# Half and transpose buffers of the latent heads in freed V memory, and the chunked outputs loaded once, in a hybrid encoder layer

## Chip, cores and metric

The kernel runs on one core of one Trainium2 chip. The metric is the device time of one execution in microseconds (us); lower is better.

## What is computed

One layer of a streaming encoder on a sequence of 1024 tokens with 1024 channels, in float32. Two groups of attention heads work on the same normalized input, their outputs are concatenated and projected, and a gated MLP follows:

```python
h = modulate(rmsnorm(x, g_attn_norm), sh_a, sc_a)
q_lat, kv_lat, k_rope, ca_qkv = split(h @ w_in)
# A: 8 latent heads, 96 wide keys, chunk-causal over all earlier keys
q = rmsnorm(q_lat) @ w_q_up;  k_nope, v = split(rmsnorm(kv_lat) @ w_kv_up)
o_mla = mla_attention(rope(rmsnorm(q)), rope(rmsnorm([k_nope, k_rope])), v)
# B: 8 chunked heads, 64 wide, a band of 9 chunks of 64 keys, relative bias
o_ca = chunk_attention(rmsnorm(cq), rmsnorm(ck), cv, rel_bias)
x = x + g_a * (concat([o_mla, o_ca]) @ w_out)
h = modulate(rmsnorm(x, g_mlp_norm), sh_m, sc_m)
gate, val = split(causal_dwconv(h @ w_up, conv_w, conv_b))
x = x + g_m * ((silu(gate) * val) @ w_down)
```

## The kernel before

The work is tiled by 128 tokens (8 tiles). Products that need float32 accuracy run as three matmuls on a high and a low part of each operand (`gemm3`): ACT makes the high part (`hi_of`, L75), POOL or DVE subtracts it for the low part (`lo_of`, L82).

A scheduler orders the instructions of each engine when the program is built, by the order in which they are issued in the source and by priorities (`tc.high_priority`); each engine then runs its own list in order and waits on semaphores. All DMAs are issued by SP's queue, transposes too, in one list. Buffers come from pools: tiles with one `tag` share `bufs` places, and a new tile waits until the last reader of the place is done.

The main loop goes over 32 units of four query tiles each: first the chunked heads (`ca_unit`, tile names ending in `c`), then the latent heads (`mla_unit`, names in `m`; `m13` is group 1, head 3). For each query tile `Unit.scores` computes q k^T into PSUM (tag S, two places), takes the row extreme on DVE (L674) and the exponential on ACT (L680) into a tile `P` (three places up to 640 keys, else a page tile with six). The probabilities are then scaled and split into two float16 halves side by side in a tile `hl`: the high half on POOL (L71), the low half on DVE (L700). One DMA transpose (L702) writes both halves, turned, into a tile `PT`. A tile of up to 640 keys is one piece, a longer one is cut in two (512 and the rest). `hl` has the tag HL with three places, `PT` the tag PT with three places. Three tiles later (`DEPTH`) `Unit.values` multiplies V with the turned halves (L713), and after four tiles ACT and DVE evict the sum and SP stores it to `oT_d` in DRAM (L720 to L722).

V of the chunked heads lies in tiles with the tag `v16` (six places of 1024 float16 for each partition), which `f_v` fills.

Between these steps the loop draws pieces of other work from a list of fillers, so that PE has matmuls while a unit waits: `pace` takes as many as a cost account asks for. The last filler is `f_oca`. It multiplies the outputs of the chunked heads (blocks 4 to 7 of `oT_d`) with their rows of `w_out` and stores the partial result to `part_d`. `load_wo` stages each weight tile through `qtile` (tag sq, two places), as the result tiles `co` are too. The input tiles come from `rtile` (tag R, four places).

After the loop, `load_wo` loads the other half of `w_out` through the same staging places, and a loop over the eight token tiles adds the latent heads' outputs (L870 to L897). The MLP stage follows.

Of the kernel before, what the change touches and what calls it, by code (L numbers as in the profile page):

```python
# [13 lines left out]
F32R = mybir.dt.float32r  # L14
F16 = mybir.dt.float16
# [8 lines left out]
P = 128  # L24
D = 1024
S = 1024
NT = S // P
# [13 lines left out]
P_BUFS, HL_BUFS, PT_BUFS, TB = 3, 3, 3, 1  # L41
# [21 lines left out]
def layer_kernel(ctx, tc, I, out):  # L63
    nc = tc.nc
    pe, act, dve, pool, sp = nc.tensor, nc.scalar, nc.vector, nc.gpsimd, nc.sync

    def f32(ap):
        return ap.bitcast(F32)
# [4 lines left out]
    def hi_of(eng, o, i):  # L73
        if eng == "a":
            act.activation(o, i, AF.Copy)  # L75
        elif eng == "p":
            pool.tensor_scalar(o, i, 1.0, 0.0, op0=MUL, op1=ADD)
        else:
            dve.tensor_copy(o, i)

    def lo_of(eng, o, i, hi):
        (pool if eng == "p" else dve).tensor_tensor(o, i, f32(hi), op=SUB)  # L82
# [3 lines left out]
    oT_d = dram.tile([ND, P, S], F32, name="oT_d")  # L86
# [37 lines left out]
    apg = att_pg.__enter__()  # L124
# [9 lines left out]
    def rtile(name, shape=(P, 512), dt=F32):  # L134
        return apg.tile(list(shape), dt, name=name, tag="R", bufs=4)

    def qtile(name):
        return apg.tile([P, 512], F32, name=name, tag="sq", bufs=2)
# [4 lines left out]
    def pgtile(shape, dt, name):  # L143
        return apg.tile(shape, dt, name=name, tag="pg", bufs=6)
# [13 lines left out]
    def gemm3_f(pt, pairs, step=GSTEP):  # L158
        n, w = len(pairs), pt.shape[-1]
        for i0 in range(0, n, step):  # L160
            part = pairs[i0:i0 + step]
            if len(trail) > LAG:
                with tc.issue_after(trail[-1 - LAG]):
                    gemm3(pt, part, i0 == 0, i0 + step >= n)
            else:
                gemm3(pt, part, i0 == 0, i0 + step >= n)
            yield 3 * len(part) * max(107, w / 2.4 + 2.5)
# [68 lines left out]
    for d in range(ND):  # L236
# [7 lines left out]
        pt = ps.tile([P, 512], F32, name=f"p_ada{d}", tag="mm", bufs=2)  # L244
# [86 lines left out]
    at = att.__enter__()  # L331
# [177 lines left out]
    def g4(shape, dt, name):  # L509
        return G["4"].tile(shape, dt, name=name, tag="G4", bufs=8)  # L510
# [72 lines left out]
    def load_wo(k0, n, he, le):  # L583
        ws = []
        for k in range(k0, k0 + 4):
            raw = qtile(f"wor{k}_{n}")
            sl = slice(n * 512, (n + 1) * 512)
            sp.dma_start(raw[:], I["w_out"][k * P:(k + 1) * P, sl])
            w = g4([P, 2, 512], F32R, f"wo{k}_{n}")
            hi_of(he, w[:, 0], raw[:])  # L590
            lo_of(le, w[:, 1], raw[:], w[:, 0])
            ws.append(w)
        return ws

    def f_oca():
        for n in range(2):
            ws = load_wo(4, n, "a", "p")
            for t in range(NT):
                lo = rtile(f"cl{t}_{n}", (P, 4, P), F32R)
                hi = rtile(f"ch{t}_{n}", (P, 4, P), F32R)  # L600
                sp.dma_start(f32(lo[:]), oT_d[4:8, :, t * P:(t + 1) * P].rearrange("k p t -> p k t"))
                hi_of("a", hi[:], f32(lo[:]))
                lo_of("p", lo[:], f32(lo[:]), hi[:])
                pt = ps.tile([P, 512], F32, name=f"oc{t}_{n}", tag="mm", bufs=2)
                yield from gemm3_f(pt[:], [(hi[:, k], lo[:, k], ws[k][:, 0], ws[k][:, 1]) for k in range(4)])
                o = qtile(f"co{t}_{n}")
                act.activation(o[:], pt[:], AF.Copy)
                sp.dma_start(part_d[t][:, n * 512:(n + 1) * 512], o[:])
# [16 lines left out]
    class Unit:  # L625
# [7 lines left out]
        def scores(u, i):  # L633

            qpg, kpgs = u.pages()
            bias = u.bias() if u.band else None
            lo = max(0, i - 4) if u.band else 0
            n = (i - lo + 1) * P
            nm = f"{u.nm}_{i}"
            rsum = cst.tile([P, 1], F32, name=f"rs{nm}", tag="rsum", bufs=4)  # L640
            ri = cst.tile([P, 1], F32, name=f"ri{nm}", tag="ri", bufs=4)
            with tc.high_priority(offset=OFF_S):
                s = ps.tile([P, 1024], F32, name=f"s{nm}", tag="S", bufs=2)
                n0 = max(0, min(4, i + 1) - lo) * P
                n1 = n - n0
                c0 = 512 - n0 if n1 else 0
                segs = [(c0, lo * P, n0, 0)] if n0 else []
                if n1:
                    segs.append((512, max(lo, 4) * P - 512, n1, 1))
                q = slice((i % 4) * P, (i % 4 + 1) * P)  # L650
                rs_ = slice(u.base, u.base + u.rows)
                for a in range(2):
                    for c, ko, w, kh in segs:
                        for b in range(2 - a):
                            last = pe.matmul(s[:, c:c + w], qpg[rs_, a, q], kpgs[kh][rs_, b, ko:ko + w],  # L655
                                             start=(a == 0 and b == 0), stop=(a == 1))
                trail.append(last.ins)
                sv = s[:, c0:c0 + n]
                m = cst.tile([P, 1], F32, name=f"m{nm}", tag="m", bufs=4)
                if u.band:  # L660
                    if i >= 4:
                        dve.memset(sv[64:128, 0:64], BIG)
                    w = min(n, 256)
                    if n > 256:
                        m0 = cst.tile([P, 1], F32, name=f"m0{nm}", tag="m0", bufs=4)
                        dve.tensor_reduce(m0[:], sv[:, :n - 256], axis=AX.X, op=MIN)
                        init = m0[:]
                    else:
                        init = 3e38
                    dve.tensor_tensor_reduce(sv[:, n - w:n], sv[:, n - w:n], bias[:, 256 - w:256], 1.0, init,  # L670
                                             ADD, MIN, accum_out=m[:])
                else:
                    dve.memset(sv[0:64, n - 64:n], BIG)
                    dve.tensor_reduce(m[:], sv, axis=AX.X, op=MIN)  # L674
                pieces = [(0, n)] if n <= 640 else [(0, 512), (512, n)]
                if n <= 640:
                    pr = at.tile([P, 640], F32, name=f"P{nm}", tag="P", bufs=P_BUFS)
                else:
                    pr = pgtile([P, 1024], F32, f"P{nm}")
                act.activation(pr[:, :n], sv, AF.Exp, bias=m[:], scale=-1.0, accum_out=rsum[:, 0:1])  # L680
            with tc.high_priority(offset=OFF_P):
                dve.reciprocal(ri[:], rsum[:, 0:1])
                dve.tensor_scalar(ri[:], ri[:], PSCALE, None, op0=MUL)  # L683
                u.pt[i] = []
                for x, (p0, p1) in enumerate(pieces):
                    w = p1 - p0
                    hl = at.tile([P, 1280], F16, name=f"hl{nm}_{x}", tag="HL", bufs=HL_BUFS)
                    pp = pr[:, p0:p1]
                    cnt[0] += 1
                    mode = (MODE_C if u.band else MODE_M)[cnt[0] % 4]  # L690
                    if mode == "2":
                        scale_pool(pp, pp, ri[:])
                        act.activation(hl[:, :w], pp, AF.Copy)
                        pool.tensor_tensor(hl[:, w:2 * w], pp, hl[:, :w], op=SUB)
                    else:
                        if mode == "1":
                            scale_pool(hl[:, :w], pp, ri[:])
                        else:
                            act.activation(hl[:, :w], pp, AF.Copy, scale=ri[:])
                        dve.scalar_tensor_tensor(hl[:, w:2 * w], pp, ri[:], hl[:, :w], op0=MUL, op1=SUB)  # L700
                    tt = at.tile([P, 10, P], F16, name=f"PT{nm}_{x}", tag="PT", bufs=PT_BUFS)
                    sp.dma_start_transpose(tt[:, :2 * w // P, :], hl[:, :2 * w])  # L702
                    u.pt[i].append((tt, lo + p0 // P, w // P))
            return sum(3 * max(107, w / 2.4) for _, _, w, _ in segs)
# [20 lines left out]
    cnt = [0]  # L725
# [88 lines left out]
    for n in range(len(tiles) + DEPTH):  # L814
        if n < len(tiles):
            u, i = tiles[n]
# [4 lines left out]
        if n >= DEPTH:  # L821
            u, i = tiles[n - DEPTH]
# [47 lines left out]
    for t in range(NT):  # L870
        lo = gb.tile([P, 4, P], F32R, name=f"ol{t}", tag="ol", bufs=3)
        hi = gb.tile([P, 4, P], F32R, name=f"oh{t}", tag="oh", bufs=3)
# [7 lines left out]
        pt = ps2.tile([P, 1024], F32, name=f"op{t}", tag="op", bufs=3)  # L880
# [268 lines left out]
```

## Time and profile before

| | us |
|---|---|
| median of three runs | 1467.54 |
| the three runs | 1464.54 to 1467.68 |
| span of the profiled execution, first to last instruction | 1461.0 |

The page gives no other time of the profiled execution than its span; the median lies 6.5 us above it. In the page PE is busy for 87% of the span, DVE 70%, POOL 53%, ACT 42%. The scores of the latent heads run from 426 to 655 us and their last products end at 676 us.

In the profile's rows, "A <- B: total, times, longest" means that A waited for B. In a group row the columns are line, engine, operation, tiles written and read, shapes and count, then busy time in us and mean ns of one, then the idle time of the engine just before and what ended it. SPq is SP's queue of DMA issues. PEclk is the granted TensorE clock as a share of full speed, and the DMA share is the mean busy share of the 16 DMA engines.

### The profile page before, as it was taken

How to read it: one execution, taken by the hardware profiler on the slowest of the kernel's cores; microseconds unless marked ns; L12 is line 12 of the kernel's file. 1: busy time of each engine (PE TensorE's matmuls, PEld its weight loads, DVE VectorE, ACT ScalarE, POOL GpSimd, SP SyncE). 2: the span in 40 equal slices, each digit the busy share in tenths (PEclk: the TensorE clock that was granted, in tenths of full speed). 3: DMA queues.
4: the chain of work that ended last, by engine and by line, in shares of the span. 5: the costliest groups of instructions: out<-in, count | busy, mean ns of one | idle time of the engine just before them, and what ended most of it. 6: DMA issues, size and time to landing. Idle time of an engine off the chain costs nothing.

```text
span 1461.0 us, 20153 instructions
## 1 busy us (share of the span) xinstructions
PE 1273.7 (87%) x6836; PEld 1053.1 (72%) x6836; DVE 1028.2 (70%) x1830; ACT 611.7 (42%) x1190; POOL 780.0 (53%) x717
## 2 busy tenths in 40 slices
PE   3859989998867788885776999999999998999997
PEld 2749878886746666764555888788888887887885
DVE  6874776476798968772487887777777777566653
ACT  4544354343455545443273434334444433332331
POOL 5263554274555745444545555566555555665662
PEclk9979987999788899996887999999999999999998
DMA  7323547455522577869611323322222234446442
GB/s 282 134 71 75 131 113 150 126 122 116 115 64 45 127 153 161 175 139 270 223 72 63 111 100 108 109 87 87 87 87 87 77 137 162 151 144 237 148 142 101
DMA packets 218595, 185.94 MB, mean 127 GB/s; under 512 B 148086, under 2 KB 183034, under 8 KB 217468
## 3 DMA queue, kind: packets, MB, share of 16 engines
q1 hardware_dynamic: 218492, 184.66, 44.0%
q8 instruction: 54, 0.88, 0.2%
q14 instruction: 49, 0.40, 0.1%
HBM read 121.17 MB, written 28.84 MB: 103 GB/s over the span
## 4 chain that ended last, share of the span: by engine, by line
PE 39%; DMA 18%; DVE 16%; POOL 12%; issue 11%; ACT 3%; SPq 1%; DVEq 0%; POOLq 0%; ACTq 0%
POOL wds L82 5%; PE p L921 4%; PE p L923 4%; PE p L922 4%; DMA aw<-w_ada 4%; DMA PTm<-hlm 3%; DMA wu<-w_up 3%; PE sc L655 3%; PE dnp L1064 2%; PE dnp L1066 2%; PE dnp L1065 2%; PE sm L655 2%; DMA PTc<-hlc 2%; DVE adacc L243 2%; DMA cl<-oT_d 1%
## 5 line engine op out<-in xcount | busy, mean ns | idle before, releaser
L82 POOL TENSOR_TENSOR wds<-wd,wds 128x512 fp32r<-128x512 f32 x88 | 153.6, 1766 | 100.7 <-ACT wds L75 100.7
L82 POOL TENSOR_TENSOR wc<-ws,wc 128x512 fp32r<-128x512 f32 x22 | 65.4, 2975 | 134.7 <-ACT wc L75 134.7
L1054 DVE TENSOR_TENSOR wd<-wd,gmbc 128x1024 f32<-128x1024 f32 x44 | 69.4, 1577 | 80.7 <-DMA wd<-w_down 78.1
L1064 PE MATMUL dnp<-wds,g 128*128 128x512 f32 x308 | 119.9, 391 | 2.8 <-DVE xo L1072 2.3
L1066 PE MATMUL dnp<-wds,g 128*128 128x512 f32 x308 | 118.5, 390 | 3.8 <-DVE g L82 3.8
L75 ACT ACTIVATE wds<-wd 128x512 fp32r<-128x512 f32 x88 | 54.8, 624 | 157.8 <-PE dnp L1066 152.7
L1065 PE MATMUL dnp<-wds,g 128*128 128x512 f32 x308 | 119.6, 389 | 0.0
L71 POOL TENSOR_SCALAR hlm<-Pm,rim 128x512 f16<-128x512 f32 (+4 forms) x88 | 66.5, 760 | 58.1 <-DMA PTm<-hlm 37.0
L71 POOL TENSOR_SCALAR hlc<-Pc,ric 128x640 f16<-128x640 f32 (+2 forms) x64 | 45.6, 715 | 79.2 <-DVE ric L683 40.1
L700 DVE SCALAR_TENSOR_TENSOR hlm<-Pm,rim,hlm 128x512 f16<-128x512 f32 (+4 forms) x88 | 66.1, 758 | 23.3 <-POOL hlm L71 23.0
L1012 DVE TENSOR_TENSOR ws<-wu,wu 128x512 f32<-128x512 f32 x22 | 28.1, 1279 | 75.6 <-DMA wu<-w_up 75.6
L655 PE MATMUL sm<-mk,mq 96*128 96x512 f32 (+3 forms) x288 | 71.1, 378 | 10.3 <-ACT Pm L680 9.3
L82 DVE TENSOR_TENSOR g<-gr,g 128x512 fp32r<-128x512 f32 x44 | 71.0, 1616 | 11.4 <-ACT g L75 11.4
L998 DVE SCALAR_TENSOR_TENSOR u<-c,pk,u 128x1023 f32<-128x1023 f32 x44 | 77.4, 1765 | 1.8 <-ACT u L997 1.8
L1033 ACT ACTIVATE u<-u 128x1024 f32<-128x1024 f32 x22 | 23.4, 1063 | 132.0 <-DVE u L999 132.0
L713 PE MATMUL pvm<-PTm,vt 128*128 128x128 f16 x576 | 49.4, 239 | 33.5 <-DMA PTm<-hlm 28.6
L680 ACT ACTIVATE Pc<-sc,mc 128x640 f32<-128x640 f32 (+2 forms) x64 | 42.2, 659 | 86.2 <-DVE mc L670 61.7
L997 ACT ACTIVATE u<-c,pk 128x1024 f32<-128x1024 f32 x44 | 52.3, 1236 | 55.2 <-DVE c L1029 55.2
L430 DVE SCALAR_TENSOR_TENSOR aacc<-aw,cs,aacc 128x256 f32<-128x256 f32 x84 | 44.7, 532 | 43.5 <-DMA aw<-w_ada 42.9
L655 PE MATMUL sc<-k,q 64*128 64x512 f32 (+3 forms) x288 | 70.1, 372 | 5.3 <-ACT Pc L680 3.0
L713 PEld LDWEIGHTS <-vt 128*128 128x128 f16 x576 | 40.6, 108 | 46.3 <-issue 41.2
L1066 PEld LDWEIGHTS dnp<-wds,g 128*128 128x128 f32 x308 | 57.8, 188 | 17.1 <-DVE g L82 5.0
(366 smaller groups left out, 4308.0 us busy)
## 6 DMA issues: line engine op xcount, KB each, us to landing
wu<-w_up SPq DMA_DIRECT2D x44, 512.0 KB, 3.9
wd<-w_down SPq DMA_DIRECT2D x44, 512.0 KB, 4.4
aw<-w_ada SPq DMA_DIRECT2D x96, 128.0 KB, 2.3
g_d<-u SPq DMA_DIRECT2D x22, 512.0 KB, 2.6
gr<-g_d SPq DMA_DIRECT2D x44, 256.0 KB, 3.6
x<-x SPq DMA_DIRECT2D x16, 512.0 KB, 8.0
adaw<-w_ada_a SPq DMA_DIRECT2D x8, 1024.0 KB, 5.6
wq_r<-w_qk SPq DMA_DIRECT2D x32, 128.0 KB, 2.5
```

What stands on the lines that cost most here:

```text
L71: pool.tensor_scalar(o, i, s, 1.0, op0=MUL, op1=MUL)
L82: (pool if eng == "p" else dve).tensor_tensor(o, i, f32(hi), op=SUB)
L655: last = pe.matmul(s[:, c:c + w], qpg[rs_, a, q], kpgs[kh][rs_, b, ko:ko + w], start=(a == 0 and b == 0), stop=(a == 1))
L700: dve.scalar_tensor_tensor(hl[:, w:2 * w], pp, ri[:], hl[:, :w], op0=MUL, op1=SUB)
L713: last = pe.matmul(u.pv[:, c], u.vst(j), mov, start=(x == 0), stop=(x == len(todo) - 1))
L921: pe.matmul(pt, sh, pg[:, 0], start=(k == 0), stop=False)
L922: pe.matmul(pt, sh, pg[:, 1], start=False, stop=False)
L998: dve.scalar_tensor_tensor(u[:, 1:], c[:, :S - 1], pk[:, cv + 1:cv + 2], u[:, 1:], op0=MUL, op1=ADD)
L1054: dve.tensor_tensor(raw[:], raw[:], gmbc[:], op=MUL)
L1064: pe.matmul(pts[t][n], sh, w[n][:, 0], start=(j == 0), stop=False)
L1065: pe.matmul(pts[t][n], sh, w[n][:, 1], start=False, stop=False)
L1066: pe.matmul(pts[t][n], sl, w[n][:, 0], start=False, stop=(j == NF - 1))
```

## The change

`f_oca` loads and splits the weights of both column halves first, and its loop over token tiles stands outside: each tile is loaded and split once and used for both halves. In `Unit.scores`, tiles of 640 keys of a latent head are cut into 512 and 128 too, and every second piece of a latent head takes its `hl` and its `PT` from the tag `v16`, six places, instead of HL and PT. There are 96 pieces of latent heads then, not 88.

```diff
     def f_oca():
-        for n in range(2):
-            ws = load_wo(4, n, "a", "p")
-            for t in range(NT):
-                lo = rtile(f"cl{t}_{n}", (P, 4, P), F32R)
-                hi = rtile(f"ch{t}_{n}", (P, 4, P), F32R)
-                sp.dma_start(f32(lo[:]), oT_d[4:8, :, t * P:(t + 1) * P].rearrange("k p t -> p k t"))
-                hi_of("a", hi[:], f32(lo[:]))
-                lo_of("p", lo[:], f32(lo[:]), hi[:])
+        ws = [load_wo(4, n, "a", "p") for n in range(2)]
+        for t in range(NT):
+            lo = rtile(f"cl{t}", (P, 4, P), F32R)
+            hi = rtile(f"ch{t}", (P, 4, P), F32R)
+            sp.dma_start(f32(lo[:]), oT_d[4:8, :, t * P:(t + 1) * P].rearrange("k p t -> p k t"))
+            hi_of("a", hi[:], f32(lo[:]))
+            lo_of("p", lo[:], f32(lo[:]), hi[:])
+            for n in range(2):
                 pt = ps.tile([P, 512], F32, name=f"oc{t}_{n}", tag="mm", bufs=2)
-                yield from gemm3_f(pt[:], [(hi[:, k], lo[:, k], ws[k][:, 0], ws[k][:, 1]) for k in range(4)])
+                yield from gemm3_f(pt[:], [(hi[:, k], lo[:, k], ws[n][k][:, 0], ws[n][k][:, 1]) for k in range(4)])
...
-                pieces = [(0, n)] if n <= 640 else [(0, 512), (512, n)]
+                short = n <= (640 if u.band else 512)
+                pieces = [(0, n)] if short else [(0, 512), (512, n)]
...
-                    hl = at.tile([P, 1280], F16, name=f"hl{nm}_{x}", tag="HL", bufs=HL_BUFS)
+                    cnt[0] += 1
+                    spare = not u.band and cnt[0] % 2
+                    if spare:
+                        hl = apg.tile([P, 1024], F16, name=f"hl{nm}_{x}", tag="v16", bufs=6)
+                    else:
+                        hl = at.tile([P, 1280], F16, name=f"hl{nm}_{x}", tag="HL", bufs=HL_BUFS)
                     pp = pr[:, p0:p1]
-                    cnt[0] += 1
...
-                    tt = at.tile([P, 10, P], F16, name=f"PT{nm}_{x}", tag="PT", bufs=PT_BUFS)
+                    if spare:
+                        tt = apg.tile([P, 8, P], F16, name=f"PT{nm}_{x}", tag="v16", bufs=6)
+                    else:
+                        tt = at.tile([P, 10, P], F16, name=f"PT{nm}_{x}", tag="PT", bufs=PT_BUFS)
                     sp.dma_start_transpose(tt[:, :2 * w // P, :], hl[:, :2 * w])
```

## The prediction

> **What bounds the kernel now.** I read the page first (span, chain), then the stretches by time, then who waited for whom in the stretch that the change touches, then the shapes of its instructions, and last the timeline of its end. The page gives the span; the three runs have their median at 1467.54 us. The page has no other time for the profiled execution, so I count the 6.5 us between as lying around the span, and apply every change in us to the median.
>
> ```profile
> span 1461.0 us, 20153 instructions
> ```
>
> The stretches (columns: us, busy PE, PEld, DVE, ACT, POOL, granted clock, DMA share, GB/s):
>
> ```profile
> 100.00:200.00 100.00, 98.90 (x784) 89.63 (x783) 61.37 (x179) 40.80 (x96) 43.48 (x57) 1.00 0.44 101
> 200.00:300.00 100.00, 94.37 (x658) 82.59 (x657) 65.06 (x195) 41.09 (x106) 43.39 (x54) 0.85 0.55 130
> 470.00:655.00 185.00, 152.94 (x1026) 122.29 (x1024) 145.63 (x374) 92.74 (x199) 97.64 (x104) 0.92 0.70 149
> 655.00:682.00 27.00, 10.67 (x88) 9.01 (x87) 10.18 (x19) 7.88 (x14) 9.51 (x11) 0.62 0.91 212
> ```
>
> The diff touches only the latent heads and the partial output product beside them. Their body is 470 to 655 us, their drain 655 to 682. In the body PE is busy 152.9 of 185 us, so 32.1 us is the most that any rearrangement can win there; DVE at 145.6 is the next limit, only 7 us better. What PE waits for, and what stands behind it (us, times, longest), in the body:
>
> ```profile
> POOL hlm L71 <- DMA PTm<-hlm: 32.3, 24, 4.1
> DVE hlm L700 <- POOL hlm L71: 19.2, 21, 3.6
> ACT Pm L680 <- DVE hlm L700: 8.1, 5, 2.5
> PE sm L655 <- ACT Pm L680: 4.8, 6, 2.2
> PE pvm L713 <- DMA PTm<-hlm: 13.6, 17, 2.0
> PE oc L150 <- ACT ch L75: 3.6, 5, 1.1
> PE oc L150 <- ACT wo L75: 1.5, 1, 1.5
> SPq L702 <- PE pvm L713: 19.8, 20, 1.4
> ```
>
> The first four rows are one chain: POOL can't write the high half of the next probabilities until a transpose has emptied one of the three HL buffers; DVE waits for POOL's half, ACT for the P buffer that DVE frees, PE's scores for ACT. The last row is the second limit of three: SP can't start a transpose until PE's value products have read a PT buffer. Together they allow three pieces between POOL and PE, and a tile of over 640 keys has two. PE pays 13.6 us (value products waiting for a transpose) and 4.8 us (scores waiting for ACT), 18.4 of its 32.1 idle us.
>
> **The change part by part.** (1) Every second piece of a latent head takes its halves and its transpose from the six V buffers, so six pieces may be under way, not three. In the built order of the changed kernel the transpose of piece 13_6_0 waits for the products of 13_2_0, six pieces back; before, it waits for 13_4_0, three back. Both limits go. What is late next is not free: the probability buffers stay at three for up to 640 keys, PE's order is fixed, and DVE is at 79%. Bounds: 0 if the next limit binds at once, -18.4 us if all waits of both rows go. Going through PE's waits in time, most come shortly behind a POOL wait of the first row, as the last of these rows does behind the one before it; the first does not, POOL was late with other work there.
>
> ```profile
> 491.83 0.61 PE L713 MATMUL pvm<-PTm,vt 128*128 128x128 f16 x8 [1.75 <-DMA PTm<-hlm]
> 646.13 0.69 POOL L71 TENSOR_SCALAR hlm<-Pm,rim 128x512 f16<-128x512 f32 x1 [3.55 <-DMA PTm<-hlm]
> 648.65 0.61 PE L713 MATMUL pvm<-PTm,vt 128*128 128x128 f16 x8 [1.25 <-DMA PTm<-hlm]
> ```
>
> I take half of 18.4: **-9.2 us**.
>
> (2) Tiles of 640 keys become pieces of 512 and 128. One form of each operation becomes two:
>
> ```profile
> L71 POOL TENSOR_SCALAR hlm<-Pm,rim 128x640 f16<-128x640 f32 x8 | 7.6, 950 | 6.0 <-ACT kraw L564 2.5 <-DVE rim L683 2.2 <-DMA PTm<-hlm 1.2
> L71 POOL TENSOR_SCALAR hlm<-Pm,rim 128x512 f16<-128x512 f32 x40 | 34.6, 866 | 25.0 <-DMA PTm<-hlm 14.9 <-DVE rim L683 4.6 <-DVE sm L673 2.2
> L71 POOL TENSOR_SCALAR hlm<-Pm,rim 128x128 f16<-128x128 f32 x8 | 3.5, 437 | 2.0 <-DVE sm L673 1.7 <-DMA PTm<-hlm 0.2
> L700 DVE SCALAR_TENSOR_TENSOR hlm<-Pm,rim,hlm 128x640 f16<-128x640 f32 x8 | 7.0, 880 | 0.2 <-POOL hlm L71 0.2
> L700 DVE SCALAR_TENSOR_TENSOR hlm<-Pm,rim,hlm 128x512 f16<-128x512 f32 x40 | 34.1, 853 | 9.9 <-POOL hlm L71 9.8
> L700 DVE SCALAR_TENSOR_TENSOR hlm<-Pm,rim,hlm 128x128 f16<-128x128 f32 x8 | 3.2, 404 | 0.8 <-POOL hlm L71 0.8
> L702 SPq DMA_TRANSPOSE PTm<-hlm x88: 1167/1238/2220, 434.1 to 671.2; - x88
> DMA to landing us min/median/max: 2.3/3.3/4.7
> ```
>
> Eight times: POOL 866+437-950 = 0.35 us, DVE 853+404-880 = 0.38 us, SP one issue of 1.24 us. That is 2.8, 3.0 and 9.9 us of engine time, between 0 (all in idle time) and 3.0 (DVE's share on the path in full; SP's 9.9 is offset below). DVE idles 39 of the 185 us; I take a third: **+1.0**. PE's products stay ten for these tiles. [...]
>
> (3) The partial product loads and splits each chunked output once:
>
> ```profile
> L601 SPq DMA_DIRECT2D cl<-oT_d x16: 372/434/653, 493.9 to 636.7; - x16
> L75 ACT ACTIVATE ch<-cl 128x512 fp32r<-128x512 f32 x16 | 10.1, 628 | 23.7 <-DMA cl<-oT_d 20.9 <-DVE qn L470 2.8
> L82 POOL TENSOR_TENSOR cl<-cl,ch 128x512 fp32r<-128x512 f32 x16 | 21.9, 1368 | 28.6 <-ACT ch L75 26.3 <-PE mq_ps L615 2.2
> ```
>
> Eight of sixteen go: ACT 5.0 us, POOL 10.9 us, SP 8 x 0.43 = 3.5 us and 2 MB of reads. All of it is beside PE's work; what PE feels is its 3.6 us wait for ch. Bounds 0 and -3.6, half: **-1.8**. In return all eight weight tiles of w_out are loaded and split ahead of the first output tile, where the second four stood in the middle. PE's wait for them is 1.5 us now; twice the row, so **+1.5** more, from 0 to the price in the slower rival.
>
> (4) The drain. SP's order there (start, us):
>
> ```profile
> 654.62 0.59 SPq L588 DMA_DIRECT2D wor<-w_out  x1
> 657.52 4.25 SPq L702 DMA_TRANSPOSE PTm<-hlm  x3
> 662.49 0.39 SPq L588 DMA_DIRECT2D wor<-w_out  x1
> 670.36 0.57 SPq L588 DMA_DIRECT2D wor<-w_out  x1
> 671.19 1.25 SPq L702 DMA_TRANSPOSE PTm<-hlm  x1
> 684.64 0.33 SPq L588 DMA_DIRECT2D wor<-w_out  x1
> 681.65 0.80 PE L150 MATMUL op<-wo,oh 128*128 128x512 f32 x1 [5.69 <-ACT oh L75]
> 692.09 1.20 DVE L82 TENSOR_TENSOR wo<-wor,wo 128x512 fp32r<-128x512 f32 x1 [2.52 <-ACT wo L75]
> ```
>
> Now the transposes at 657.52 stand for a PT buffer. Without that wait they start at 655.2 and nine of them (one is the new piece) at 1.24 us end near 666.4, not at 672.4: the last value product comes some 6 us sooner. But the output projection that follows ends on the last weight tile, split at 692 to 693. The loads for it take turns in two staging buffers: from 670.36 to 684.64 five steps, 2.86 us each. In the changed order the second load no longer stands among the transposes (662.49) but behind all of them and two stores: about 668. Six steps of 2.86 put the last at 685, where it was. So the 6 us are won and lost again: between -6 and +2, I take **-0.5**.
>
> Sum: -9.2 + 1.0 - 1.8 + 1.5 - 0.5 = -9.0. Span 1452, median 1467.5 - 9.0 = **1458.5 us**. Everything after 705 us keeps its order.
>
> **The rivals.**
>
> [...] Chance 0.13.
>
> *The transfers are the bound*: six pieces under way only queue in the DMA engines.
>
> ```profile
> DMA packets 5154, 1.80 MB, mean 180 GB/s; under 512 B 4865, under 2 KB 4865, under 8 KB 5153
> q1 hardware_dynamic: 5153, 1.78, 96.6%
> ```
>
> These are 660 to 670 us: six transposes and three small transfers fill the 16 engines at only 180 GB/s. The body's mean share of 0.70 leaves room between bursts, and part 3 takes 2 MB away; inside bursts it may not. Then the gain is 0 to -3: about 1466. [...] Chance 0.15.
>
> *Slower: weights at the head of SP's queue.* The loads of the second four weight tiles now stand among the transposes of the second and third latent head (about 500 to 525 us), each waiting for POOL to free a staging buffer, with the transposes behind it.
>
> ```profile
> SPq L588 <- POOL wo L82: 4.9, 2, 2.9
> L82 POOL TENSOR_TENSOR wo<-wor,wo 128x512 fp32r<-128x512 f32 x12 | 17.7, 1480 | 12.3 <-ACT wo L75 12.3
> wor<-w_out SPq DMA_DIRECT2D x9, 256.0 KB, 3.3
> ```
>
> Four such waits at the longest seen, 2.9 us, are 11.6 us in which no transpose starts; PE meets its first product with them soon after and stands too. It decides if a load, its two halves (ACT's as for ch above) and POOL's queue take more than a turn of (3.3 + 0.6 + 1.5) / 2 = 2.7 us. With half of part 1 won: +11.6 - 4.6 = +7, 1474.5. For it: SP is held at such loads already. Against: the built order spreads those products over six tiles. Chance 0.21.
>
> *It does not do what it says*: the next limit (three P buffers, DVE) binds at once: 1467. Chance 0.06. The forecast keeps 0.45, with 1452 to 1464 as its own range.
>
> **How the numbers follow.** A measurement here tells 0.2%, 3 us, from no change. Faster: 0.45 + 0.13 and a part of the DMA case, 0.60. Slower: the SP case and a little, 0.22. Same: 0.18. The range goes from 1446, half into the larger gain, to 1472, short of the slower case's middle; it leaves out about 0.07 below and 0.13 above.
>
> **What would show it.** Right: POOL's wait for PTm falls from 32.3 to under 12, SP's wait for pvm from 19.8 to under 6, PE idles under 25 us in the body, the drain's last product comes sooner without the first op product's end moving. Wrong: PE's wait for PTm stays over 10 with the DMA share over 0.8 (transfers), or SP's wait at the w_out loads exceeds 8 us near 510 (weights), or DVE passes 85% with PE idle as before.

## The result, and the profile after

The changed kernel takes 1457.5 us (median; 1456.2 to 1460.0), the kernel before 1466.2 us in the same comparison (1462.2 to 1471.6): a ratio of 0.9938, 95% interval 0.9917 to 0.9959, or 9.1 us. A second comparison, on another occasion, gave 0.9935 (0.9916 to 0.9954). The forecast was 1458.5 us.

The page's first line and the stretches by time of the changed kernel (columns as in the prediction: us, busy PE, PEld, DVE, ACT, POOL, granted clock, DMA share, GB/s):

```profile
span 1454.4 us, 20116 instructions
```

```profile
470.00:655.00 185.00, 155.16 (x1083) 126.44 (x1083) 154.56 (x404) 93.63 (x202) 95.27 (x113) 0.93 0.73 147
655.00:682.00 27.00, 15.87 (x79) 12.61 (x79) 4.73 (x5) 6.79 (x11) 11.94 (x10) 0.62 0.93 262
```

More work fits into the same 185 us (PE 155.2 us against 152.9, DVE 154.6 against 145.6), and the drain holds more of PE's work (15.9 against 10.7 us), since the output projection begins inside it now.

Who waited for whom in the body (470 to 655 us), changed kernel (us, times, longest):

```profile
POOL hlm L71 <- DVE rim L684: 39.7, 21, 4.8
ACT Pm L681 <- DVE mm L674: 21.2, 16, 4.2
PE pvm L721 <- DMA PTm<-hlm: 9.9, 12, 2.3
PE sm L655 <- ACT Pm L681: 5.6, 9, 1.8
DVE hlm L705 <- POOL hlm L71: 5.3, 10, 0.9
PE oc L150 <- ACT ch L75: 0.7, 1, 0.7
PE oc L151 <- POOL wo L82: 2.1, 2, 1.4
PE oc L150 <- ACT wo L75: 0.2, 1, 0.2
SPq L710 <- PE pvm L721: 11.5, 13, 1.2
SPq L588 <- POOL wo L82: 2.0, 1, 2.0
```

The row that headed the chain, POOL waiting for a transpose to free its halves (32.3 us), is gone. In its place POOL and ACT wait for DVE. SP's wait for PE's value products is down from 19.8 to 11.5 us.

One caution on absolute times: the first latent score product starts between 424.3 and 430.1 us in thirteen of the fourteen profiles of this study, with almost the same program ahead of it (the fourteenth, e7 below, changes that program). So I count from that product. The rows on PE that give the marks, before and then after:

```profile
426.05 0.49 PE L655 MATMUL sm<-mk,mq 96*128 96x128 f32 x2 [0.77 <-ACT mk L621]
654.32 1.61 PE L655 MATMUL sm<-mk,mq 96*128 96x512 f32 x6
674.95 1.01 PE L713 MATMUL pvm<-PTm,vt 128*128 128x128 f16 x8 [1.71 <-DMA PTm<-hlm]
```

```profile
429.99 0.50 PE L655 MATMUL sm<-mk,mq 96*128 96x128 f32 x2 [0.77 <-ACT mk L621]
648.06 1.63 PE L655 MATMUL sm<-mk,mq 96*128 96x512 f32 x6
663.16 1.87 PE L721 MATMUL pvm<-PTm,vt 128*128 128x128 f16 x16 [3.14 <-DMA PTm<-hlm]
670.50 0.79 PE L150 MATMUL op<-wo,oh 128*128 128x512 f32 x1 [5.47 <-ACT oh L75]
```

So the last score product ends 229.9 us behind the first start in the kernel before and 219.7 us in the changed one. The same marks for every kernel that ran (us from the first score product; each from one profile; ratios to before with 95% intervals):

| kernel | last score | last value | first output proj. | last output proj. | end of span | ratio |
|---|---|---|---|---|---|---|
| before | 229.9 | 249.9 | 255.6 | 316.7 | 1035.0 | 1 |
| changed | 219.7 | 235.0 | 240.5 | 304.4 | 1024.4 | 0.9938 (0.9917–0.9959) |
| changed, again (ctl_after) | 219.4 | 234.6 | 240.4 | 304.1 | 1022.7 | 0.9935 (0.9916–0.9954) |
| e1_buffers | 219.6 | 234.9 | 251.6 | 314.6 | 1033.3 | 0.9987 (0.9970–1.0004) |
| e10_prio | 222.8 | 238.5 | 244.0 | 307.4 | 1027.9 | 0.9973 (0.9954–0.9992) |
| e2_once | 226.7 | 246.6 | 252.0 | 312.5 | 1030.3 | 0.9984 (0.9963–1.0005) |
| e3_split | 231.4 | 253.5 | 259.3 | 314.5 | 1032.1 | 0.9989 (0.9969–1.0009) |
| e4_nosplit | 217.3 | 232.1 | 237.6 | 300.1 | 1020.3 | 0.9903 (0.9875–0.9930) |
| e4 again (ctl_nosplit) | 216.6 | 231.2 | 236.4 | 299.3 | 1017.6 | 0.9889 (0.9861–0.9917) |
| e5_hl | 222.4 | 251.5 | 256.5 | 320.1 | 1039.0 | 1.0030 (1.0016–1.0044) |
| e6_pt | 227.2 | 244.4 | 248.7 | 307.8 | 1025.8 | 0.9952 (0.9935–0.9969) |
| b2_pt | 233.1 | 249.0 | 253.5 | 317.3 | 1036.4 | 0.9997 (0.9980–1.0014) |
| e7_rope | 215.9 | 231.3 | 237.9 | 302.0 | 1019.6 | 0.9941 (0.9921–0.9961) |
| b1_rope | 216.3 | 230.4 | 236.1 | 300.1 | 1018.0 | 0.9874 (0.9849–0.9899) |

Read along the second row against the first: 10.2 us won in the body, 14.9 by the last value product, 12.3 left after the output projection, 10.6 at the end of the span, 9.1 by the ratio of the runs.

### The profile page after: what moved, and what is told of

Its sections match the earlier page's. It is cut to its first block, busy times and chain, and to the rows that moved or that the text cites. A ratio compares the mean times of both kernels' runs of the same rounds, so it can differ in the third digit from the quotient of the medians.

```text
span 1454.4 us, 20116 instructions
## 1 busy us (share of the span) xinstructions
PE 1270.4 (87%) x6836; PEld 1054.4 (72%) x6836; DVE 1029.9 (71%) x1838; ACT 606.5 (42%) x1182; POOL 770.3 (53%) x717
## 4 chain that ended last, share of the span: by engine, by line
PE 23%; POOL 9%; DVE 8%; issue 8%; DMA 7%; ACT 1%; SPq 1%; DVEq 0%; POOLq 0%; ACTq 0%
PE p L929 5%; PE p L931 5%; PE p L930 5%; POOL wds L82 5%; DMA wu<-w_up 2%; PE dnp L1072 2%; PE dnp L1074 2%; PE dnp L1073 2%; DVE u L1007 1%; DMA wd<-w_down 1%; DVE ws L1020 1%; DVE u L1006 1%; POOL wf L82 1%; POOL we L82 1%; POOL wd L82 1%
## 5 line engine op out<-in xcount | busy, mean ns | idle before, releaser
L71 POOL TENSOR_SCALAR hlm<-Pm,rim 128x512 f16<-128x512 f32 (+3 forms) x96 | 64.8, 685 | 78.9 <-DVE rim L684 39.7
L655 PE MATMUL sm<-mk,mq 96*128 96x512 f32 (+3 forms) x288 | 71.2, 377 | 10.2 <-ACT Pm L681 6.7
L655 PE MATMUL sc<-k,q 64*128 64x512 f32 (+3 forms) x288 | 68.7, 365 | 10.7 <-ACT Pc L681 6.8
L705 DVE SCALAR_TENSOR_TENSOR hlm<-Pm,rim,hlm 128x512 f16<-128x512 f32 (+3 forms) x96 | 68.5, 727 | 6.1 <-POOL hlm L71 5.9
L1074 PEld LDWEIGHTS dnp<-wds,g 128*128 128x128 f32 x308 | 58.2, 189 | 18.0 <-DVE g L82 5.9
L1072 PEld LDWEIGHTS dnp<-wds,g 128*128 128x128 f32 x308 | 58.1, 189 | 15.1 <-DVE xo L1080 2.6
```

The costliest lines, as they stand in the source:

```text
L71: pool.tensor_scalar(o, i, s, 1.0, op0=MUL, op1=MUL)
L1072: pe.matmul(pts[t][n], sh, w[n][:, 0], start=(j == 0), stop=False)
L1074: pe.matmul(pts[t][n], sl, w[n][:, 0], start=False, stop=(j == NF - 1))
```

## The experiments

The first question was which part carries the gain. The theory on trial was the forecast's: the two limits of three buffers. The rival was the single load of the chunked outputs.

**e1_buffers**: the buffers and the split, with the old partial product.

```
-        ws = [load_wo(4, n, "a", "p") for n in range(2)]
-        for t in range(NT):  ...  for n in range(2):
+        for n in range(2):
+            ws = load_wo(4, n, "a", "p")
+            for t in range(NT):
```

> Only the buffers and the split of 640-key tiles are changed; the partial product still loads and splits each chunked output twice. Medians so far 1466.2 us before and 1457.5 after, 8.7 us apart. Theory (the limit of three half buffers and three transpose buffers was what cost): my terms for it are -9.2 + 1.0 - 0.5 = -8.7, so about 1457.5 us, POOL's wait for the transposes gone as in the changed kernel. Rival (the saved loads and splits of the chunked outputs are what helped: 10.9 us less of POOL, 5.0 of ACT, 2 MB less): about 1465 us, nearly the time before. If both share it by halves: 1462 us.

Measured 0.9987: 1459.6 us beside 1461.8. That is the rival's time (1.2 us less was expected by it, 1.9 came by the ratio); the theory's 8.7 us lie outside the interval. Yet POOL's wait for the transposes is gone, and up to the last value product the marks are those of the changed kernel (234.9 and 235.0 us). But the same marks do not stand for the same work here. The matmuls of the partial product (oc) on PE up to the last score product, before and then e1 (us, busy PE and count, granted clock, DMA share, GB/s):

```profile
426.00:656.00 230.00, 56.65 (x187) 0.90 0.61 130
```

```profile
426.00:646.05 220.05, 46.08 (x156) 0.87 0.63 130
```

Of the 192 matmuls of the partial product, e1 leaves 36 for the time behind its last score product and 12 for the time behind its last value product. The kernel before and the changed one leave 5 and none. So the marks of e1 show the buffers too well: its shorter body holds less work. And the first output projection comes 11 us later than in the changed kernel. The PE timeline of e1 says why:

```profile
659.36 2.06 PE L721 MATMUL pvm<-PTm,vt 128*128 128x128 f16 x30
666.31 0.80 PE L150 MATMUL oc<-wo,ch 128*128 128x512 f32 x1 [4.90 <-ACT ch L75]
678.08 1.65 PE L150 MATMUL op<-wo,oh 128*128 128x512 f32 x3 [5.17 <-ACT wo L75]
```

All value products are done, and then a partial product still waits 4.9 us for its halves. Seven of the eight weight tiles for the output projection, which pass the same two staging buffers as the partial results, are loaded only behind it:

```profile
677.99 13.20 SPq L588 DMA_DIRECT2D wor<-w_out  x7
```

In this kernel's built order the last of the sixteen partial products begins behind all 576 value products; in the changed kernel it begins behind 504.

**e2_once**: the new partial product with the old buffers (the other half of the diff).

> Only the partial product is changed (each chunked output loaded and split once, all eight weight tiles ahead); halves and transposes keep three buffers each, 640-key tiles stay whole. Theory: -1.8 + 1.5 = -0.3 us, about 1466 us, within 0.2% of before, with POOL's wait for transposes still near 32 us in the body. Rival (saved loads are the gain): 1458 to 1460 us. Third possibility (the weight loads hold back transposes that are already short of buffers): 1469 us or more, with SP's wait at the weight loads above the 4.9 us of before.

Measured 0.9984, 2.3 us by the ratio, its interval from 0.9963 to just above 1. That is the theory's side. The load at the head of SP's queue, my slower rival, is not seen: SP waits 3.2 us at the weight loads in the body, where it waited 2.9. With three buffers still in force POOL waits longer than before, and yet the time does not grow.

```profile
POOL hlm L71 <- DMA PTm<-hlm: 53.4, 30, 5.3
PE pvm L713 <- DMA PTm<-hlm: 13.3, 15, 2.0
```

Alone the two parts give 1.9 us and 2.3 us; together they give 9.5 (0.9935). The gap of 5.3 us is only just wider than the three intervals allow together (4.8 us, an estimate from their widths). And e1 is not the buffers with everything else kept, since its partial product falls behind. e10 below puts that product back, and then the parts nearly add up.

**e3_split** and **e4_nosplit** try the 640-key split by itself: alone on the kernel before, and taken out of the changed kernel.

```
-                pieces = [(0, n)] if n <= 640 else [(0, 512), (512, n)]
+                short = n <= (640 if u.band else 512)
+                pieces = [(0, n)] if short else [(0, 512), (512, n)]
```

> Only the split of 640-key tiles into 512 and 128: 88 transposes become 96, all in three buffers. Theory (each piece holds one of three places): the split costs by itself more than the 1.0 us of the prediction, since eight more pieces stand in the same three places: 1 to 4 us over before, 1467 to 1470 us. Rival (smaller pieces come sooner to TensorE, so the split is part of the gain): 1463 us or less.

```
-                short = n <= (640 if u.band else 512)
+                short = n <= 640
...
-                    spare = not u.band and cnt[0] % 2
+                    spare = not u.band and cnt[0] % 2 and w <= 512
```

> The changed kernel without the split: 640-key tiles stay one piece and take the three large buffers, the odd pieces of up to 512 keys take the V buffers. Theory (split costs 1.0 us, six places are enough): 1456.5 us, 0 to 2 us under the changed kernel's 1457.5. Rival (the split was needed so that pieces take turns between the two sets of buffers; two or more neighbours in the same set of three wait again): 1460 us, with a wait of POOL for transposes of 5 us or more back in the body.

e3 came out at 0.9989, inside an interval that holds no change, where 1 to 4 us of loss were expected. Its marks show the loss and where it is made good: the last value product is 3.6 us later than before, but the output projection is 5.9 us shorter (55.2 against 61.1 us). That fits with its weights, which came in during the longer drain (the last at 685.5 us, 3.4 behind the last value product; before, at 684.6, 8.7 behind it). e4 is the best of the first set: 0.9903, and **ctl_nosplit**, the same kernel, gave 0.9889 later.

> The kernel without the split once more, as the measure for the variants beside it. Its first ratio was 0.9903 with an interval of 0.9875 to 0.993, the changed kernel's 0.9935 (0.9916 to 0.9954). Theory (the split costs 3.0 us of DVE, 2.8 of POOL and 9.9 of SP and buys nothing): 0.990 to 0.992 again. Rival (the difference was noise): 0.993 or more.

That is the theory's side, a little under its range. The split therefore costs, and more than I counted: 2.9 and 3.4 us at the last value product (two profiles each), 5 to 7 us by the ratios. Single intervals still touch or overlap a little; the four together give 5.9 us, give or take 3.5 (an estimate from their widths). The groups by shape, changed kernel, then the kernel without the split (count | busy us, mean ns):

```profile
L705 DVE SCALAR_TENSOR_TENSOR hlm<-Pm,rim,hlm 128x512 f16<-128x512 f32 x48 | 41.5, 867 | 3.7 <-POOL hlm L71 3.5
L705 DVE SCALAR_TENSOR_TENSOR hlm<-Pm,rim,hlm 128x128 f16<-128x128 f32 x16 | 7.3, 454 | 0.2 <-POOL hlm L71 0.2
L710 SPq DMA_TRANSPOSE PTm<-hlm x96: 1167/1234/2886, 437.8 to 658.7; - x96
```

```profile
L705 DVE SCALAR_TENSOR_TENSOR hlm<-Pm,rim,hlm 128x512 f16<-128x512 f32 x40 | 34.6, 865 | 2.8 <-POOL hlm L71 2.7
L705 DVE SCALAR_TENSOR_TENSOR hlm<-Pm,rim,hlm 128x640 f16<-128x640 f32 x8 | 6.9, 866 | 0.3 <-POOL hlm L71 0.2
L705 DVE SCALAR_TENSOR_TENSOR hlm<-Pm,rim,hlm 128x128 f16<-128x128 f32 x8 | 3.4, 429 | 0.0
L710 SPq DMA_TRANSPOSE PTm<-hlm x88: 1167/1242/2161, 432.2 to 651.3; - x88
```

DVE has 48.8 against 44.9 us of this work, SP eight issues more.

**ctl_after, e5_hl, e6_pt** ask which of the two limits holds. In e5 only the halves take turns with the V buffers, in e6 only the transposed pieces. The kind that takes turns then has all six V places to itself.

```
 e5:                if False:      # in place of "if spare:" ahead of tt
 e6:                if False:      # in place of "if spare:" ahead of hl
```

> The changed kernel as it is, beside its variants: the measure for the three other kernels of this set. From the first comparison (0.9938 of before) it should stand 7 to 11 us under before here too; the kernel without the split stood at 0.9903 of before on another occasion, so the difference between those two is only known to about 5 us.

> The changed kernel, but only the halves alternate between the two sets (six buffers); the transposed pieces all stay in the three PT buffers. Theory (POOL's wait for a free HL buffer, 32.3 us before, and SP's wait for a free PT buffer, 19.8 us, are two limits of three in one chain; a transpose that cannot start keeps its halves): the smaller part of the gain, ratio to before 0.997 to 1.0, with SP's wait for the value products near 20 us again. Rival (the first limit, the halves, is all): same as the changed kernel within 0.2%.

> The changed kernel, but only the transposed pieces alternate (six buffers); the halves stay in three HL buffers. Theory (the transposes start as soon as the halves are there, so an HL buffer is held only for DVE's half and the transfer of 2.3 to 4.7 us): the larger part of the gain, ratio to before 0.994 to 0.997, with some 10 to 15 us of POOL's wait for PT back. Rival (POOL's wait for HL buffers, 32.3 us, was the limit and stays): no gain, ratio 0.998 to 1.0, that wait at 30 us or more.

For e6 the ratio is as the theory had it (0.9952, three quarters of the gain), but POOL's wait is as the rival had it (41.7 us, over 30); e5 is worse than expected (1.0030, slower than before). The waits of e5, then of e6:

```profile
POOL hlm L71 <- DMA PTm<-hlm: 29.7, 17, 4.8
SPq L710 <- PE pvm L721: 24.8, 19, 2.4
```

```profile
POOL hlm L71 <- DMA PTm<-hlm: 41.7, 31, 3.6
PE pvm L721 <- DMA PTm<-hlm: 12.8, 13, 2.4
```

With more halves and three transposed pieces the scores run ahead (222.4 us), but the value products cannot follow: 465 of the 576 are done by the last score product, where the kernel before had 504. SP waits longer than before for PE to free a PT buffer, and 29.1 us lie between the last score and the last value product, against 20.0. What the scores gain is lost behind them. In e6 POOL waits even longer than before (41.7 against 32.3 us), and the kernel is faster: that wait, the longest row of the view, is no measure of the cost.

**b2_pt** is e6 without the split.

> Only the transposes of pieces of up to 512 keys alternate with the V buffers, the halves keep their three, 640-key tiles stay whole, chunked outputs loaded once. Theory (the transposed pieces are the limit, the halves are not; the split costs some): between the kernel with both sets and no split (0.9903) and the transposes-only kernel with the split (0.9952): 0.991 to 0.993. Rival (with whole 640-key pieces more neighbours share the three halves): 0.995 or more.

A clear miss of the theory: 0.9997, no gain, in the rival's range. The rival's reason is not borne out either, since POOL waits less for the transposes than in e6:

```profile
POOL hlm L71 <- DMA PTm<-hlm: 25.6, 14, 4.1
```

Its last score product is the latest of all (233.1 us). So "the transposed pieces alone are the limit" does not stand either. What stands is coarser, and holds for all fourteen profiles: with both limits lifted the last value product ends 230.4 to 238.5 us behind the first score product; with either one left at three, 244.4 to 251.5; with both left, 246.6 to 253.5. The last two ranges overlap, so at that mark lifting one limit is not told from lifting none. Why e6 and b2 differ by 4.6 us at that point is open: each edit also makes the scheduler write another order, and no run was made with the order held fixed.

**e10_prio** goes back to e1's miss and lifts the loads and halves of the chunked outputs in the scheduler's priority.

```
+                with tc.high_priority(offset=200):
+                    sp.dma_start(f32(lo[:]), oT_d[4:8, ...])
+                    hi_of("a", hi[:], f32(lo[:]))
+                    lo_of("p", lo[:], f32(lo[:]), hi[:])
```

> The kernel with the buffers and the split alone (each chunked output still loaded and split twice), with the loads and halves of the chunked outputs raised by 200 in the scheduler's priority. In the buffers-only kernel the built order left the last 3 of the 16 partial products behind all score products, the last one behind all value products, and its last product ended at 672.6 us, 11 us behind the last value product; now the last starts with 504 of 576 value products issued, as in the changed kernel. Theory (the buffers won 10 us in the body and this tail gave them back): ratio to before 0.994 to 0.996, near the changed kernel's 0.9935. Rival (the second load and split themselves cost, 10.9 us of POOL and 5.0 of ACT): 0.998 to 1.0 as in the buffers-only kernel's 0.9987.

Measured 0.9973, between the two, with an interval that reaches into both ranges. The tail is gone: 5.6 us from the last value product to the output projection, where e1 had 16.7, and as many matmuls of the partial product in the body as before (187). But the body is 3.2 us longer than e1's, with PE's scores waiting 9.8 us for ACT, where e1 had 4.8:

```profile
PE sm L656 <- ACT Pm L682: 9.8, 9, 1.8
```

So the tail explains part of what e1 lost. By the marks 7.2 us of it come back at the last output projection, 5.4 at the end of the span; the ratios differ by 0.14%, less than their intervals. What still parts e10 from the changed kernel, 3.1 us in the body, is the second set of loads and splits, or the built order, which differs too. The two theories share the verdict.

With the partial product in its place, the two parts of the diff add up. In the body the single load alone gives 3.2 us (e2), the buffers with the split give 7.1 (e10, with its raised priority), and both give 10.2. At the last value product it is 3.3, 11.4 and 14.9. (These are single profiles; two profiles of one kernel differ by up to 0.9 us at these marks.) By the ratios 2.3 and 4.0 us make 6.3 of the 9.1 to 9.5, and the rest is inside the intervals.

**e7_rope** and **b1_rope** ask whether DVE, which POOL and ACT now wait for, sets the pace.

```
 e7:  rope_apply(..., tabq, t, 4, rq[:, 0:256])                          # was: dve
 b1:  rope_apply(..., tabq, t, 4, rq[:, 0:256], pool if gr else dve)     # on the kernel without the split
```

> The changed kernel with the four rotary operations per token tile of the latent queries (0.425 + 0.370 + 0.246 + 0.208 us = 1.25 us on DVE, eleven times between 430 and 650 us, 13.7 us) moved from DVE to POOL. DVE is busy 187 of those 220 us, POOL 112. Theory (DVE is the limit that took over in the body): 3 to 8 us under the changed kernel. Rival (DVE is late only because its order is fixed, and POOL's halves are queued behind the rotary operations now): the same or 2 to 6 us slower, with more waits of DVE for POOL's halves.

> The kernel without the split, with the rotary operations of the latent queries moved from DVE to POOL for the second group of heads only. In the kernel with all of them moved, first to last score product took 216.0 us against 219.3, but the first score product came 22.1 us behind the last chunked value product against 17.5. Theory (moving only the second group keeps the first and leaves out the second): 2 to 4 us under the kernel without the split, ratio to before 0.987 to 0.989. Rival (DVE is not what sets the body's pace): the same as the kernel without the split.

e7 gave 0.9941 beside 0.9935: no gain. The body is 3.5 us shorter than the changed kernel's beside it, but POOL pays for it ahead of the body (the stretch from 412 to 470 us, changed kernel, then e7: POOL 27.2 and 47.7 us busy), and the first score product starts 22.1 us behind the last chunked value product, not 17.4 to 19.0 as in the two profiles of the changed kernel.

```profile
412.00:470.00 58.00, 41.48 (x188) 32.93 (x189) 52.21 (x172) 34.15 (x83) 27.19 (x32) 0.81 0.18 42
```

```profile
412.00:470.00 58.00, 41.19 (x197) 32.41 (x197) 48.87 (x132) 33.34 (x83) 47.71 (x75) 0.84 0.18 39
```

b1 leaves the first group on DVE: 1445.4 us beside 1446.9 (0.9874 and 0.9889), 1.4 us and well inside both intervals. Its body is 216.3 us against 216.6. DVE as the next limit is not shown. The kernel without the split is the one to keep: 1.0 to 1.1% under the kernel before, where the changed kernel is 0.62 to 0.65% under it.

## Why the prediction came out, step by step

The sum was -9.0 us and the medians gave -8.7, the ratio -9.1. Its terms did not all earn it: the split cost more than its term and the single load gave more than its terms, and the two errors partly cancel. That the sum hit so closely is luck.

**Term 1, the buffers (-9.2).** Right in place and in sign, and in size by luck. With the single load in both kernels, the buffers without the split shorten the body by 9.4 and 10.1 us (from e2 to e4 and to ctl_nosplit). With the split it is 7.0 us (from e2 to the changed kernel), or 7.1 with the old loads in both (from before to e10); terms 1 and 2 had 8.2. But the two PE rows that I halved fell far less than by half. In the body's fixed stretch they went from 13.6 + 4.8 to 9.9 + 5.6 us. Summed from the first to the last score product, they fell by 4.9, 3.5, 3.3 and 1.1 us in the four comparisons above, about half of the gain at best. From before to the changed kernel PE's idle time went from 44.9 to 38.6 us. Its busy time, which I had taken as fixed, went from 185.1 to 181.4, for the same score products, two more matmuls of the partial product and twelve more value products:

```profile
426.00:656.00 230.00, 185.05 (x1186) 148.24 (x1187) 186.28 (x507) 119.21 (x263) 120.54 (x131) 0.90 0.61 130
```

```profile
430.00:650.00 220.00, 181.40 (x1200) 147.95 (x1200) 186.96 (x515) 115.84 (x257) 112.07 (x132) 0.91 0.64 129
```

So half of those rows was a fair price, but the rows are not where most of the gain shows. Which waits and products hold the rest is open.

**Term 2, the split (+1.0).** Mis-sized, and the weakest step. I let a third of DVE's 3 us count and nothing of SP's eight issues. The runs show 2.4 and 2.8 us in the body, 2.9 to 3.6 at the last value product, with six places (e4) and with three (e3), and 5 to 7 us in the ratio with six. How much of it is DVE's and how much SP's is not shown.

**Term 3, the single load (-1.8 + 1.5).** Mis-sized: -0.3 was forecast, and the body shows -3.2 (e2) and -3.1 us (from e10 to the changed kernel). The ratio of e2 alone, -2.3 us, does not exclude -0.3. The step that failed is the price of the two rows. In e2 PE's wait for ch goes whole, from 3.6 us to none, not by half; its wait for the weights goes from 1.5 to 1.7 us and not up by 1.5. In the changed kernel the two stand at 0.7 and 2.3 us. I also did not ask what a shorter body does to the old partial product. In e1 its built order falls behind the value products, and the gain comes back at the output projection; from e1 to the changed kernel the single load is worth 7.6 us by the ratio.

**Term 4, the drain (-0.5).** Right in the net (10.2 us won at the last score product and 10.6 at the end of the span; 10.5 and 12.3 in ctl_after), off in the place. The last score to the last value product went from 20.0 to 15.3 us, 4.7 of the 6 forecast. But the first output product did not keep its time, as I had said it would; it moved with the value products (5.5 us behind them, 5.7 before). What ended late was the last weight tile:

```profile
676.16 7.52 SPq L588 DMA_DIRECT2D wor<-w_out  x3
686.67 0.69 DVE L82 TENSOR_TENSOR wo<-wor,wo 128x512 fp32r<-128x512 f32 x1 [2.74 <-ACT wo L75]
```

Before, that tile was split at 693.3 us, 267 us behind the first score product; here at 687.4, 257: the 10 us of the body and nothing of the drain. The output projection is longer by 2.7 us (63.8 against 61.1, from first to last product).

**The announced signs.** POOL's wait for PTm fell from 32.3 to none (under 12 was asked): right. SP's wait for pvm fell to 11.5, not under 6: wrong, yet the kernel gained. My reading is that what is left of this wait stood at pieces that no value product was short of; no run tests it. PE's idle time in the fixed body window is 29.8 us, not under 25; counted from first to last score it fell by 6.3. None of the three signs against came, the first only just: 9.9 us (over 10 was asked) and 0.73 for the transfers, 2.0 us at the weight loads, DVE at 84%.

**The rivals.** *The larger gain* (chance 0.13): no. Of the 18.4 us of waits that part 1 counts, 15.5 (9.9 + 5.6) still stand in the fixed stretch. The lower end of the range, 1446, rests in part on a higher clock in the body, and the rows show none above 0.93: it is 0.92 in the kernel before (PE busy 152.9 of 185 us), 0.93 in the changed one (155.2 of 185) and 0.91 in e7 from 470 to 650 us (155.5 of 180). *Transfers are the bound*: not in the body, where their mean share is 0.73, after 0.70; in the drain they nearly fill the engines. From 655 to 665 us of the changed kernel:

```profile
DMA packets 4467, 1.69 MB, mean 169 GB/s; under 512 B 4145, under 2 KB 4145, under 8 KB 4465
q1 hardware_dynamic: 4465, 1.66, 94.8%
```

The one queue takes 94.8% of the engines' time at 169 GB/s, as it took 96.6% at 180 in the kernel before, from 660 to 670 us. *Slower by the weight loads*: not seen in any run with the new partial product. Its nearest relative was e1, where the weights at the end, not those in the middle, were what came late.

## What to carry to other kernels

Two buffers that follow each other in one chain have to be tested each alone and both together, before the longer wait is believed. Here one alone gave a loss of 0.3%, a gain of 0.5% and no change, and both gave 0.6 to 1.1%. A mark in time compares two kernels only if the same work lies ahead of it; count the instructions first. A term priced by an engine's wait in the old kernel holds for the old pace only: ask of every side task (here the partial product and its weights) whether it can still keep up when the main loop is faster. Smaller pieces that a buffer size forces can cost nearly all of their engine time, not a third of it (here 3.9 us more on DVE, and 2.4 to 3.6 at the marks); see first whether the large pieces can stay where they are.

## What the runs showed of the chip that I had not expected

The rotary operations cost POOL 704, 555, 423 and 356 ns in e7 where DVE took 425, 370, 246 and 208 in the changed kernel: 2.04 us a token tile against 1.25, a factor of 1.6. Almost the same instructions ahead of the change put the first score product anywhere from 424.3 to 430.1 us, a spread of more than half of the effect, so that medians of many runs and marks counted from a common point were needed to see it. The profiled execution of the changed kernel had 1.8 us around its span (1456.2 and 1454.4), and so had the later runs of the kernel before (1466.5 and 1464.7 in one of them). So of the 6.5 us that I counted for the kernel before, some 4.7 were by estimate (6.5 less 1.8) a profiled run faster than the median.
